# A written issue order for three engines, from the output projection to the FFN's activation sums

## The chip, the core and the metric

The kernel runs on one core of one Trainium2 chip. The core's engines are TensorE (PE: matrix products and transposes into eight PSUM banks of 128 x 512 float32), VectorE (DVE), ScalarE (ACT), GpSimd (POOL), and SyncE (SP), whose queue issues the DMAs. Each engine works through its own list of instructions in order, and semaphores tie the lists together. The metric is the time of one execution on the device in microseconds (us), the median of several runs.

## What is computed

One decoder layer over 1024 tokens of width 1024, in float32. Attention and a gated convolution each give 512 columns; these are normalised, projected, added to x, normalised again and sent through a gated FFN of width 2816. The part around the change:

```python
m = jnp.concatenate([rmsnorm(a, attn_group_norm[i]),
                     rmsnorm(c, conv_group_norm[i])], axis=-1)
x = x + rmsnorm(m @ w_out[i], mix_post_norm[i])
h = rmsnorm(x, ffn_pre_norm[i])
f = (jax.nn.silu(h @ w_gate[i]) * (h @ w_up[i])) @ w_down[i]
x = x + rmsnorm(f, ffn_post_norm[i])
```

with `rmsnorm(x, g) = x * rsqrt(mean(x * x) + 1e-6) * g` over the last axis.

## The kernel before

**Products.** Every float32 matrix is kept as two float32r parts, h (the rounded value, a cast by ScalarE) and l (the rest, a subtraction by VectorE); `split` (L195) makes them. A product is three matmuls per block, h·h, h·l and l·h. So each operand that reaches TensorE costs a ScalarE and a VectorE instruction first. In the FFN, `factor` (L1100) makes the weight's parts for one product and `product` (L1132) is 12 matmuls and the reading of the bank.

**The FFN's seven products.** The FFN's first stage takes the 2x2 blocks of the weights and of the activations and forms seven products in place of eight (Strassen's scheme in Winograd's form). They come in the order p = 1, 2, 6, 5, 7, 3, 4 for each pair fp of weight tiles and for m = 0 (gate) and m = 1 (up). Products 1 and 2 need the activation blocks B11 and B21, which hold the first 512 tokens. Products 3, 5, 6 and 7 need B22 and the sums T1, T2 and T3, which need all tokens; product 4 needs T4. The sums are chained: T3 = B22 - B12, T2 = T3 + B11, T1 = B22 - T2, T4 = B21 - T2. Each is 128 x 2048 and is split when it is done. Products 1 and 2 of fp = 0, 1 and 2 are therefore put ahead of the rest, as work for TensorE while the sums are made.

**The rows before that.** The output projection works on eight tiles t of 128 tokens. For each tile:

- `wo_a` (L1018): 24 matmuls for the attention half (`wo_half`) into two banks; VectorE scales the result and adds the convolution half y, which was written to DRAM earlier (L1021); ScalarE squares the row and sums it (L219, in a helper); the helper `rstd_of` adds epsilon on VectorE (L215) and takes the power -1/2 on GpSimd (L216).
- `wo_x1` (L1025): VectorE normalises (L1027), adds x (L1029); the row is stored to x1_d (L1031); a second square and power for the next norm.
- `wo_n` (L1034): VectorE normalises in place (L1036). As it overwrites the row that is stored to x1_d, it waits until that store has landed.
- `h2_turn` (L1046): TensorE transposes the tile (8 transposes, L1056) into two banks, ScalarE copies them, ScalarE and VectorE split them into B11 and B21 (first four tiles) or B22 (last four). The first four tiles' plain copies go to hr_d in DRAM and are read back later, since T2 and T4 need them; the last four tiles' plain copies stay in `tr`.

The tile loop (L1204) writes these steps staggered: wo_a of tile t, wo_x1 of t - 1, wo_n of t - 2, h2_turn of t - 3.

**Memory.** `mf` is one array of 30 units of 128 x 512 float32. A buffer takes the free units that were freed longest ago; what the last user of the units still does, a new user has to wait for. `raw_load` (L1094) asks for the gate and up weights of one fp and one half. t2, a buffer of its own (four units), holds T2 and then T4, while b12 holds T3.

**What sets the order.** The program is traced into one sequence; the framework's scheduler then gives each engine its list, from a timeline that it reckons itself while compiling, and adds the semaphores. The written sequence is a priority, not an order: an instruction written later may be put ahead on its engine. So it was with the four weight factors that are written at t = 4 (L1237), which were put ahead of the loop.

Of the kernel before, what the change touches and what calls it, by code (L numbers as in the profile page):

```python
# [42 lines left out]
D = 1024  # L43
# [89 lines left out]
def hybrid_layer(ctx: ExitStack, tc: tile.TileContext, x, x_t, p_t, cols_in, positions,  # L133
# [79 lines left out]
    def rstd_of(ss, n=1):  # L213

        dve.tensor_scalar_add(ss, ss, EPS)  # L215
        pool.tensor_tensor(ss, ss, mhalf[:, 0:n], op=ALU.pow)  # L216

    def mean_sq(junk, src, n, ss):
        act.activation(junk, src, AF.Square, scale=float(n) ** -0.5, accum_out=ss)  # L219
# [713 lines left out]
    def wo_half(t, m, k0):  # L933
        ids, b = ps.get(2)
        for n in range(2):
            o = slice(n * U, (n + 1) * U)
            mm3(b[:, o], [(m[j][0].a[:, t * P : (t + 1) * P], m[j][1].a[:, t * P : (t + 1) * P],
                           wo[k0 + j][0].a[:, o], wo[k0 + j][1].a[:, o]) for j in range(4)])
        return ids, b
# [68 lines left out]
        rows_x[t] = mf(2, ML)  # L1008
        sp.dma_start(rows_x[t].a, x[t * P : (t + 1) * P, :])

    def row_norm(t, i):
# [4 lines left out]
        rstd_of(r)

    def wo_a(t):  # L1018
        y = rows_y[t].a
        ids, b = wo_half(t, mTa, 0)  # L1020
        dve.scalar_tensor_tensor(y, b, ss_a[:, t : t + 1], y, op0=ALU.mult, op1=ALU.add)  # L1021
        ps.put(ids)
        row_norm(t, 0)

    def wo_x1(t):  # L1025
        y, xr = rows_y[t].a, rows_x.pop(t)
        dve.scalar_tensor_tensor(y, y, ss_y[:, 2 * t : 2 * t + 1], g_mix.a, op0=ALU.mult,  # L1027
                                 op1=ALU.mult)
        dve.tensor_tensor(y, y, xr.a, op=ALU.add)  # L1029
# [13 lines left out]
    def four(b):  # L1043
        return b.a.rearrange("p (k c) -> p k c", k=4)

    def h2_turn(t):  # L1046
# [5 lines left out]
        for q in range(2):  # L1052
            ids, b = ps.get()
            for j in range(4):
                k = 4 * q + j
                pe.transpose(b[:, j * P : (j + 1) * P], src.a[:, k * P : (k + 1) * P], ident[:])  # L1056
# [4 lines left out]
            if first or q:  # L1061
                h, l = tf["B" + "12"[q] + "12"[not first]]
                split(four(h)[:, :, o], four(l)[:, :, o], bank3(b, 4))
            ps.put(ids)
# [65 lines left out]
    blk, bank = {}, {}  # L1130

    def product(fp, m, p):  # L1132
        key = fp, m, {1: "X", 6: "X", 7: "X", 4: "X", 2: "Z", 5: "Y", 3: "Y"}[p]
# [5 lines left out]
        first, last = p in (1, 2, 5), p in (2, 3, 4)  # L1139
        for k in range(4):  # L1140
            c = slice(k * P, (k + 1) * P)
            pe.matmul(b, wh.a[:, c], th[:, k], start=first and k == 0, stop=False,  # L1142
                      skip_group_check=True)
            pe.matmul(b, wh.a[:, c], tl[:, k], start=False, stop=False, skip_group_check=True)  # L1144
            pe.matmul(b, wl.a[:, c], th[:, k], start=False, stop=k == 3, skip_group_check=True)  # L1145
        free(wh, wl)

        c = {1: "11", 2: "11", 6: "12", 3: "12", 5: "22", 7: "22", 4: "21"}[p]
        if p in (1, 6, 5, 4):
            blk[fp, m, c] = mf(1)  # L1150
        o = blk[fp, m, c].a
        g = blk[fp, 0, c].a
        if p in (1, 6, 5):
            act.copy(o, b)
        elif p == 4 and m == 0:
            act.activation(o, b, AF.Silu)
        elif p == 4:
            dve.tensor_tensor(o, b, g, op=ALU.mult)
        else:
            dve.tensor_tensor(o, b, o, op=ALU.add)  # L1160
            if m == 0:
                act.activation(o, o, AF.Silu)
# [40 lines left out]
    head = [(0, m, p) for p in (1, 2) for m in range(2)]
    for t in range(T + 3):  # L1204
        if t < T:
            wo_a(t)
        elif t == T:
            for d in (mTa, wo):
                for h, l in d.values():
                    free(h, l)  # L1210
            for i in head[:2]:
                product(*i)
        elif t == T + 1:
            for i in head[2:]:
                product(*i)
        if 1 <= t <= T:
            wo_x1(t - 1)
        if t < T:
            load_x(t)
        if 2 <= t <= T + 1:  # L1220
            wo_n(t - 2)
        if t == T + 1:
            free(g_mix, g_ffn)
            t2 = mf(4, MG)
            tf["T1"], tf["T4"] = pair(4, BT), pair(4, BT)
            b11, b21 = tf["T1"][1].a.bitcast(F32), tf["T4"][1].a.bitcast(F32)
            sp.dma_start(b11.rearrange("p (k c) -> p k c", k=4), hr_d[:, 0:4, :])
            sp.dma_start(b21.rearrange("p (k c) -> p k c", k=4), hr_d[:, 4:8, :])
        if t >= 3:
            h2_turn(t - 3)  # L1230
        if t + 2 < T:
            load_y(t + 2)
        if t == T - 1:
            raw_load(0, 1, ML)
        if t == T:
            raw_load(1, 0, ML)
        if t == T // 2:  # L1237
            for i in head:
                factor(*i)
    b12, b22 = tr[0], tr[1]  # L1240
# [14 lines left out]
    t_sum(b12.a, b22.a, b12.a, ALU.subtract)
    both(factor, 1, 1)
    both(product, 1, 1)
    t_sum(t2.a, b12.a, b11, ALU.add)
    t_split("T3", b12.a)
    free(b12)  # L1260
    raw_load(2, 0)
    both(factor, 1, 2)
    both(product, 1, 2)
    t_split("T2", t2.a)
    both(factor, 0, 6)
    t_sum(b22.a, b22.a, t2.a, ALU.subtract)
    both(factor, 2, 1)
    both(product, 2, 1)
    t_split("T1", b22.a)
    free(b22)  # L1270
    both(factor, 2, 2)
    both(product, 2, 2)
# [295 lines left out]
```

## Time and profile before

| | |
|---|---|
| Median of 3 runs | 1228.94 us (1228.4 to 1229.56) |
| The profiled execution: its time, its span from first to last instruction | 1231.37 us, 1229.6 us |
| TensorE busy (matmuls) | 1196.8 us, 97% of the span |
| VectorE busy | 818.5 us, 67% |
| ScalarE busy | 584.8 us, 48% |
| GpSimd busy | 514.6 us, 42% |
| DMA | 215.68 MB, mean 175 GB/s |
| TensorE's granted clock, mean | 0.993 of full speed |

How to read it: the page of a profile lists busy times, the chain of work that ended last and the costliest groups of instructions. The trace behind it can be asked for single stretches of time: a timeline gives start, duration, engine, line of the kernel, what is written and read, and in brackets how long the engine stood idle before and what it waited for. `mem_f` and `mem_r` are the arrays of plain values and of split parts, `banks` is PSUM, `small` holds the row sums. L198 is the cast of `split`, L199 its subtraction, L209 to L211 the projection's matmuls, L1142 to L1145 the FFN's, L1154 to L1164 the reading of the FFN's banks. Matmuls are pipelined, so a matmul that lasts 0.39 us starts 0.23 us after the one before.

The stage of the change lies from about 441 us (the projection's first matmuls) to about 549 us.

### The profile page before, as it was taken

To read this page: it belongs to the slowest core of one execution; us is meant where nothing else is said; L and a number is where in the kernel's file an instruction comes from. 1 tells how busy PE (TensorE), PEld (TensorE's weight loads), DVE (VectorE), ACT (ScalarE), POOL (GpSimd) and SP (SyncE) were. 2 spreads that over 40 slices of the span, in tenths; PEclk is the share of its full clock that TensorE was granted. 3 is DMA by queue.
4 is the path that set the end of the run, shared out by engine and by line. 5 is a ranking of instruction groups with operands and counts; after the bars stand their busy time and mean duration, and the time that the engine had idled before them with its cause. 6 is when DMAs were issued, how large, how long until landed. Compare 5 with 4: busy or idle time off the path is not lost.

```text
span 1229.6 us, 16643 instructions
## 1 busy us (share of the span) xinstructions
PE 1196.8 (97%) x5902; PEld 1009.4 (82%) x5902; DVE 818.5 (67%) x1171; ACT 584.8 (48%) x1071; POOL 514.6 (42%) x391
## 2 busy tenths in 40 slices
PE   7899999999999999889999999999999999999998
PEld 5898888889989887678788888888888888888876
DVE  6954357568866757895757755564657577758675
ACT  6543322357766735643423433333344556545552
POOL 5523545216554312125887745864723012203231
PEclk9999999999999999889999999999999999999999
DMA  6522653894561658624565435534656567654341
GB/s 243 181 70 82 200 205 117 266 380 87 135 164 53 224 195 267 221 103 138 183 226 197 133 133 205 180 126 144 218 189 205 188 216 246 212 189 157 120 141 74
DMA packets 88941, 215.68 MB, mean 175 GB/s; under 512 B 8918, under 2 KB 17402, under 8 KB 87546
## 3 DMA queue, kind: packets, MB, share of 16 engines
q1 hardware_dynamic: 88800, 214.60, 52.5%
q8 instruction: 46, 0.75, 0.3%
q14 instruction: 37, 0.30, 0.1%
q10 hardware_dynamic: 58, 0.02, 0.0%
HBM read 143.28 MB, written 71.04 MB: 174 GB/s over the span
## 4 chain that ended last, share of the span: by engine, by line
PE 78%; DVE 7%; DMA 6%; issue 4%; POOL 2%; ACT 2%; SPq 1%; POOLq 0%; ACTq 0%; DVEq 0%
PE banks L1142 10%; PE banks L1144 10%; PE banks L1145 10%; PE banks L1339 6%; PE banks L1341 6%; PE banks L1340 6%; PE banks L209 5%; PE banks L211 5%; PE banks L210 5%; PE banks L844 2%; DVE mem_r L199 2%; PE banks L815 2%; PE banks L811 1%; PE banks L1451 1%; PE banks L1448 1%
## 5 line engine op out<-in xcount | busy, mean ns | idle before, releaser
L199 DVE TENSOR_TENSOR mem_r<-mem_f,mem_r 128x512 fp32r<-128x512 f32 (+3 forms) x401 | 376.6, 969 | 214.7 <-ACT mem_r L198 201.7
L198 ACT CAST mem_r<-mem_f 128x512 fp32r<-128x512 f32 (+1 forms) x404 | 258.0, 670 | 384.5 <-PE banks L1144 117.9
L1142 PE MATMUL banks<-mem_r 128*128 128x512 f32 x616 | 242.1, 394 | 5.9 <-ACT mem_r L198 5.1
L1144 PE MATMUL banks<-mem_r 128*128 128x512 f32 x616 | 242.2, 393 | 3.0 <-DVE mem_r L199 3.0
L1145 PE MATMUL banks<-mem_r 128*128 128x512 f32 x616 | 241.3, 393 | 0.0
L210 PE MATMUL banks<-mem_r 128*128 128x512 f32 (+2 forms) x536 | 196.6, 368 | 1.4 <-POOL mem_r L199 1.4
L209 PE MATMUL banks<-mem_r 128*128 128x512 f32 (+2 forms) x536 | 195.5, 371 | 1.0 <-DVE small L215 0.4
L211 PE MATMUL banks<-mem_r 128*128 128x512 f32 (+2 forms) x536 | 196.0, 367 | 0.0
L1142 PEld LDWEIGHTS banks<-mem_r 128*128 128x128 f32 x616 | 116.8, 190 | 32.5 <-ACT mem_r L198 6.5
L1144 PEld LDWEIGHTS banks<-mem_r 128*128 128x128 f32 x616 | 117.1, 190 | 27.5 <-DVE mem_r L199 3.5
L1145 PEld LDWEIGHTS banks<-mem_r 128*128 128x128 f32 x616 | 117.0, 190 | 25.1 <-DVE mem_r L199 0.7
L1341 PE MATMUL banks<-mem_r 128*128 128x512 f32 x308 | 119.8, 389 | 0.0
L1339 PE MATMUL banks<-mem_r 128*128 128x512 f32 x308 | 119.8, 390 | 0.0
L1340 PE MATMUL banks<-mem_r 128*128 128x512 f32 x308 | 119.8, 389 | 0.0
L210 PEld LDWEIGHTS banks<-mem_r 128*128 128x128 f32 x536 | 101.2, 189 | 17.9 <-POOL mem_r L199 2.1
L209 PEld LDWEIGHTS banks<-mem_r 128*128 128x128 f32 x536 | 100.7, 189 | 17.7 <-ACT mem_r L198 0.7
L211 PEld LDWEIGHTS banks<-mem_r 128*128 128x128 f32 x536 | 101.0, 189 | 16.1
L829 POOL TENSOR_TENSOR mem_f<-mem_f,stats 128x640 f32<-128x640 f32 (+5 forms) x64 | 72.5, 1146 | 92.2 <-DVE stats L825 45.4
L216 POOL TENSOR_TENSOR small<-small,mhalf 128x1 f32<-128x1 f32 (+2 forms) x42 | 40.8, 972 | 155.3 <-DVE small L215 152.3
L1160 DVE TENSOR_TENSOR mem_f<-banks,mem_f 128x512 f32<-128x512 f32 x66 | 45.2, 686 | 51.5 <-PE banks L1145 51.4
L199 DVE TENSOR_TENSOR mem_r<-banks,mem_r 128x512 fp32r<-128x512 f32 (+3 forms) x118 | 69.2, 612 | 10.9 <-ACT mem_r L198 10.2
L198 ACT CAST mem_r<-banks 128x512 fp32r<-128x512 f32 (+3 forms) x118 | 58.8, 536 | 25.1 <-PE banks L844 13.7
(194 smaller groups left out, 1895.7 us busy)
## 6 DMA issues: line engine op xcount, KB each, us to landing
sc_d<-mem_f SPq DMA_DIRECT2D x77, 256.0 KB, 2.6
mem_f<-sc_d SPq DMA_DIRECT2D x77, 256.0 KB, 3.2
mem_f<-in_w_gate_dram SPq DMA_DIRECT2D x22, 512.0 KB, 5.2
mem_f<-in_w_up_dram SPq DMA_DIRECT2D x22, 512.0 KB, 3.9
mem_f<-in_w_down_dram SPq DMA_DIRECT2D x22, 512.0 KB, 4.2
wc_d<-mem_f SPq DMA_DIRECT2D x22, 512.0 KB, 2.8
mem_f<-wc_d SPq DMA_DIRECT2D x44, 256.0 KB, 3.6
mem_f<-in_w_down_dram SPq DMA_DIRECT2D x33, 256.0 KB, 3.5
```

Source lines behind the costliest of these rows:

```text
L198: act.copy(h, src)
L199: (eng or dve).tensor_tensor(l, src, h.bitcast(F32), op=ALU.subtract)
L209: pe.matmul(o, wh, vh, start=i == 0, stop=False)
L210: pe.matmul(o, wh, vl, start=False, stop=False)
L211: pe.matmul(o, wl, vh, start=False, stop=i == n - 1)
L829: pool.tensor_tensor(pt.a[:, 0:n], pt.a[:, 0:n], sm.to_broadcast([P, n]), op=ALU.mult)
L1142: pe.matmul(b, wh.a[:, c], th[:, k], start=first and k == 0, stop=False, skip_group_check=True)
L1144: pe.matmul(b, wh.a[:, c], tl[:, k], start=False, stop=False, skip_group_check=True)
L1145: pe.matmul(b, wl.a[:, c], th[:, k], start=False, stop=k == 3, skip_group_check=True)
L1339: pe.matmul(b, ah.a[:, c], bh.a, start=first, stop=False, skip_group_check=True)
L1340: pe.matmul(b, ah.a[:, c], bl.a, start=False, stop=False, skip_group_check=True)
L1341: pe.matmul(b, al.a[:, c], bh.a, start=False, stop=last, skip_group_check=True)
```

## The change

From the projection's loop to T4's split, everything stands in one `manual_schedule` region for TensorE, VectorE and ScalarE: their instructions go out in the order in which they are written. GpSimd and SP are scheduled as before. For that the steps are cut into parts that belong to one engine, and written anew as `wo_step`:

```diff
+    def wo_step(t, fill=()):
+        if t < T:
+            wo_mm(t)
+        if t >= 3:
+            turn_act(t - 3)
+        if 1 <= t <= T:
+            wo_a(t - 1)
+        if 2 <= t <= T + 1:
+            row_rstd(t - 2, 1)
+        for i in fill:
+            factor(*i)
+        if t >= 3:
+            turn_dve(t - 3, 0)
+        if 2 <= t <= T + 1:
+            wo_n(t - 2)
+        if 1 <= t <= T:
+            row_rstd(t - 1, 0)
+        if t >= 3:
+            turn_dve(t - 3, 1)
+            turn_put(t - 3)
+        if 2 <= t <= T + 1:
+            turn_pe(t - 2)
+        if 1 <= t <= T:
+            wo_x1(t - 1)
+        if t < T:
+            load_x(t)
+        if t + 2 < T:
+            load_y(t + 2)
```

`wo_mm` is the 24 matmuls; `wo_a` what VectorE does with them and ScalarE's square; `row_rstd` epsilon and power; `turn_pe` the eight transposes; `turn_act` all of ScalarE's copies of a turned tile (for a tile of the first four: two rounded parts, then two plain copies and the store to hr_d; for one of the last four: one rounded part and two plain copies); `turn_dve` the subtraction of one of its two banks; `wo_x1` ends with ScalarE's second square. The four factors of fp = 0, p = 1 and 2, are the `fill` of steps 4 to 7, one each. `product` is cut into its matmuls (`product_mm`) and the reading of the bank (`product_end`). What follows the loop is written out:

```diff
+        for t in range(T):
+            wo_step(t, {4: ((0, 0, 1),), 5: ((0, 1, 1),), 6: ((0, 0, 2),), 7: ((0, 1, 2),)}
+                    .get(t, ()))
...
+        raw_load(0, 1, ML)
+        both(product_mm, 0, 1)
+        wo_step(T)
+        raw_load(1, 0, ML)
+        both(product_end, 0, 1)
...
+        both(product_mm, 0, 2)
+        wo_step(T + 1)
+        free(g_mix, g_ffn)
+        raw_load(2, 0, ((0, 22),))
+        product_end(0, 0, 2)
+        factor(1, 0, 1)
+        product_mm(1, 0, 1)
+        factor(1, 1, 1)
+        product_end(0, 1, 2)
+        product_mm(1, 1, 1)
+        factor(0, 0, 6)
+        turn_act(T - 1)
+        turn_dve(T - 1, 1)
+        turn_put(T - 1)
+        both(product_end, 1, 1)
+        b12, b22 = tr[0], tr[1]
+        t_sum(b12.a, b22.a, b12.a, ALU.subtract)
+        factor(1, 0, 2)
+        product_mm(1, 0, 2)
+        factor(1, 1, 2)
+        product_mm(1, 1, 2)
+        t_split("T3", b12.a)
+        factor(2, 0, 1)
+        product_end(1, 0, 2)
+        product_mm(2, 0, 1)
+        t_sum(b12.a, b12.a, b11, ALU.add)
+        factor(2, 1, 1)
+        product_mm(2, 1, 1)
+        product_end(1, 1, 2)
+        t_split("T2", b12.a)
+        both(product_end, 2, 1)
+        factor(2, 0, 2)
+        product_mm(2, 0, 2)
+        factor(2, 1, 2)
+        product_mm(2, 1, 2)
+        factor(0, 1, 6)
+        t_sum(b22.a, b22.a, b12.a, ALU.subtract)
+        product_end(2, 0, 2)
+        t_split("T1", b22.a)
+        product_end(2, 1, 2)
+        free(b22)
+        both(factor, 0, 5)
+        t_sum(b12.a, b21, b12.a, ALU.subtract)
+        factor(0, 0, 7)
+        t_split("T4", b12.a)
```

The sums: t2 is gone; b12 holds T3, then T2, then T4, each written over the one before. The four units that t2 had are free, and raw_load(2, 0) stands ahead of the sums, where before it stood behind T3's split. raw_load(0, 1) moves from tile T - 1 to behind the loop, raw_load(1, 0) from tile T to behind step T.

More of the change, by code (lines that the diff above doesn't have):

```diff
@@ L1044, in four, with turn_pe, turn_places, turn_act @@
         return b.a.rearrange("p (k c) -> p k c", k=4)
-    def h2_turn(t):
+    turned = {}
+    def turn_pe(t):
         src = rows_y.pop(t)
-        o = slice(t % 4 * P, (t % 4 + 1) * P)
+        turned[t] = [ps.get(), ps.get()]
+        for q, (ids, b) in enumerate(turned[t]):
+            for j in range(4):
+                k = 4 * q + j
+                pe.transpose(b[:, j * P : (j + 1) * P], src.a[:, k * P : (k + 1) * P], ident[:])
+        free(src)
+    def turn_places(t):
+        o = slice(t % 4 * P, (t % 4 + 1) * P)
+        for q, (ids, b) in enumerate(turned[t]):
+            if t < T // 2 or q:
+                h, l = tf["B" + "12"[q] + "12"[t >= T // 2]]
+                yield q, b, four(h)[:, :, o], four(l)[:, :, o]
+    def turn_act(t):
+        o = slice(t % 4 * P, (t % 4 + 1) * P)
+        for q, b, h, l in turn_places(t):
+            act.copy(h, bank3(b, 4))
         first = t < T // 2
@@ L1051, in h2_turn @@
             raw = mf(2, ML)
[L1052 to L1056, printed above, removed]
+        for q, (ids, b) in enumerate(turned[t]):
             if first:
@@ L1060, in h2_turn @@
                 act.copy(four(tr[q])[:, :, o], bank3(b, 4))
[L1061 to L1064, printed above, removed]
         if first:
@@ L1067, in h2_turn, with turn_dve, turn_put @@
             free(raw)
-        free(src)
+    def turn_dve(t, only):
+        for q, b, h, l in turn_places(t):
+            if q == only:
+                dve.tensor_tensor(l, bank3(b, 4), h.bitcast(F32), op=ALU.subtract)
+    def turn_put(t):
+        for ids, b in turned.pop(t):
+            ps.put(ids)
     for t in range(NW, T):
@@ L1138, in product @@
         th, tl = (four(v) for v in tf[RIGHT[p]])
-        first, last = p in (1, 2, 5), p in (2, 3, 4)
+        first = p in (1, 2, 5)
         for k in range(4):
@@ L1146, in product, with product_end @@
         free(wh, wl)
+    def product_end(fp, m, p):
+        key = (fp, m, {1: "X", 6: "X", 7: "X", 4: "X", 2: "Z", 5: "Y", 3: "Y"}[p])
+        ids, b = bank[key]
         c = {1: "11", 2: "11", 6: "12", 3: "12", 5: "22", 7: "22", 4: "21"}[p]
@@ L1164, in product @@
                 dve.tensor_tensor(o, o, g, op=ALU.mult)
-        if last:
+        if p in (2, 3, 4):
             ps.put(ids)
@@ L1202, in hybrid_layer @@
     tr[0], tr[1] = mf(4, ((22, 26),)), mf(4, ((26, 30),))
[L1203 to L1240, printed above, removed]
     def both(f, fp, p):
@@ L1253, in t_sum @@
         dve.tensor_tensor(o, x, y, op=op)
[L1255 to L1272, printed above, removed]
@@ new lines, in hybrid_layer @@
+    EN = mybir.EngineType
+    with tc.manual_schedule(engines={EN.PE, EN.DVE, EN.Activation}):
+        for t in range(T):
+            wo_step(t, {4: ((0, 0, 1),), 5: ((0, 1, 1),), 6: ((0, 0, 2),), 7: ((0, 1, 2),)}
+                    .get(t, ()))
+        for d in (mTa, wo):
+            for h, l in d.values():
+                free(h, l)
+        raw_load(0, 1, ML)
[3 more added lines that the diff above has]
+        both(product_end, 0, 1)
+        tf["T1"], tf["T4"] = pair(4, BT), pair(4, BT)
+        b11, b21 = tf["T1"][1].a.bitcast(F32), tf["T4"][1].a.bitcast(F32)
+        sp.dma_start(b11.rearrange("p (k c) -> p k c", k=4), hr_d[:, 0:4, :])
+        sp.dma_start(b21.rearrange("p (k c) -> p k c", k=4), hr_d[:, 4:8, :])
+        both(product_mm, 0, 2)
[43 more added lines that the diff above has]
+        t_split("T4", b12.a)
+        free(b12)
```

25 lines of the change are left out of this document (13 added, 12 removed).

## The prediction

> **What bounds the kernel now.** First the window view over the stages that the change touches: stretch, us, each engine's busy time (TensorE, its weight loads, VectorE, ScalarE, GpSimd), TensorE's granted clock, DMA share and GB/s.
>
> ```profile
> 441.00:488.00 47.00, 47.00 (x228) 39.29 (x227) 36.16 (x47) 19.44 (x37) 10.49 (x12) 1.00 0.65 209
> 488.00:535.00 47.00, 36.66 (x147) 28.57 (x146) 40.40 (x47) 28.62 (x46) 5.03 (x5) 0.85 0.50 180
> 535.00:549.00 14.00, 14.00 (x63) 11.56 (x62) 11.31 (x12) 7.53 (x11) 3.42 (x3) 1.00 0.30 106
> ```
>
> TensorE never stops during the output projection (441 to 488) nor from 535 on. Between, it is busy 36.66 of 47 us at a clock of 0.85. What ended the stops is in TensorE's timeline and the view of waits (total, times, longest); how it ran after them, in the window view again:
>
> ```profile
> 485.66 0.39 PE L209 MATMUL banks<-mem_r 128*128 128x512 f32 x1
> ...
> 487.48 0.39 PE L211 MATMUL banks<-mem_r 128*128 128x512 f32 x1
> 489.51 0.73 PE L1142 MATMUL banks<-mem_r 128*128 128x512 f32 x2 [0.76 <-ACT mem_r L198]
> ...
> 528.70 0.79 PE L1142 MATMUL banks<-mem_r 128*128 128x512 f32 x1 [3.08 <-ACT mem_r L198]
> ```
> ```profile
> PE banks L1144 <- DVE mem_r L199: 3.0, 1, 3.0
> PE banks L1056 <- DVE mem_f L1036: 2.2, 1, 2.2
> ```
> ```profile
> 493.30:496.50 3.20, 3.20 (x8) 2.52 (x9) 3.20 (x4) 1.15 (x2) 0.00 (x0) 0.50 0.38 108
> 510.90:513.80 2.90, 2.90 (x7) 2.22 (x8) 2.90 (x5) 2.52 (x5) 0.00 (x0) 0.51 0.46 184
> 528.70:534.20 5.50, 5.50 (x13) 4.33 (x14) 5.50 (x5) 2.68 (x3) 0.00 (x0) 0.50 0.00 0
> ```
>
> Eight matmul starts from 485.66 to 487.48 make 0.228 us each. After each stop of 2 to 3 us the clock stood at half: 28 matmuls in 11.6 us, 6.4 at full clock. After the stop of 0.76 us it did not (two in 0.73). Idle 10.3, half-clock stretches 5.2 and ragged restarts (an estimate of 1.5) make **17 us lost**. That is all the change can win: 1229 - 17 = 1212.
>
> VectorE's timeline shows the kind of fault:
>
> ```profile
> 491.93 0.69 DVE L1112 TENSOR_TENSOR mem_f<-mem_f 128x512 f32<-128x512 f32 x1 [3.00 <-DMA mem_f<-in_w_gate_dram]
> 492.54 0.68 DVE L199 TENSOR_TENSOR mem_r<-banks,mem_r 128x512 fp32r<-128x512 f32 x1
> ```
>
> The subtraction at 492.54, for which TensorE stood 3.0 us, sat behind a factor's sum that waited for a weight. An engine does nothing past its next instruction. The new order is just as fixed, so I read it for the same fault.
>
> **The change part by part.** The instructions are the same, the four sums too; order and places change. I walk the three written lists with durations from these rows: timelines of VectorE, ScalarE and GpSimd, groups with their mean ns, the DMA view and x1_d's landings, TensorE's chain.
>
> ```profile
> 439.98 2.50 DVE L199 TENSOR_TENSOR mem_r<-mem_f,mem_r 128x512 fp32r<-128x512 f32 x4 [5.09 <-ACT mem_r L198]
> ...
> 446.31 1.28 DVE L1021 SCALAR_TENSOR_TENSOR mem_f<-banks,small,mem_f 128x1024 f32<-128x1024 f32 x1 [2.43 <-PE banks L211]
> 448.81 0.16 DVE L215 TENSOR_SCALAR small<-small 128x1 f32<-128x1 f32 x1 [1.22 <-ACT mem_r L219]
> 449.63 1.28 DVE L1027 SCALAR_TENSOR_TENSOR mem_f<-mem_f,small 128x1024 f32<-128x1024 f32 x1 [0.66 <-DMA y_d<-mem_f]
> 450.95 1.23 DVE L1029 TENSOR_TENSOR mem_f<-mem_f 128x1024 f32<-128x1024 f32 x1
> ...
> 455.92 1.28 DVE L1036 SCALAR_TENSOR_TENSOR mem_f<-mem_f,small 128x1024 f32<-128x1024 f32 x1 [1.18 <-DMA x_d<-mem_f]
> ...
> 481.51 1.28 DVE L199 TENSOR_TENSOR mem_r<-banks,mem_r 128x512 fp32r<-128x512 f32 x2
> ```
> ```profile
> 464.26 1.06 ACT L219 ACTIVATE mem_r<-mem_f 128x1024 fp32r<-128x1024 f32 x1 [2.29 <-DVE mem_f L1029]
> ...
> 468.17 0.22 ACT L219 ACTIVATION_READ_ACCUMULATOR mem_r<-mem_f 128x1 f32 x1
> ```
> ```profile
> 481.68 0.54 POOL L216 TENSOR_TENSOR small<-small,mhalf 128x1 f32<-128x1 f32 x1 [3.33 <-DVE small L215]
> ```
> ```profile
> L199 DVE TENSOR_TENSOR mem_r<-mem_f,mem_r 128x512 fp32r<-128x512 f32 x17 | 11.6, 704 | 0.1
> L198 ACT CAST mem_r<-mem_f 128x512 fp32r<-128x512 f32 x15 | 9.0, 620 | 13.6 <-PE banks L1144 8.1 <-DMA mem_f<-in_w_up_dram 3.5 <-DVE mem_f L1118 1.7
> L1154 ACT COPY mem_f<-banks 128x512 f32<-128x512 f32 x8 | 4.6, 581 | 4.0 <-PE banks L1145 4.0
> L1160 DVE TENSOR_TENSOR mem_f<-banks,mem_f 128x512 f32<-128x512 f32 x6 | 4.1, 685 | 1.9 <-PE banks L1145 1.9
> L1162 ACT ACTIVATE mem_f<-mem_f 128x512 f32<-128x512 f32 x3 | 1.9, 629 | 0.3 <-DVE mem_f L1160 0.3
> L1162 ACT ACT_TABLE_LOAD x1 | 1.3, 1283 | 0.0
> ```
> ```profile
> x_d<-mem_f SPq DMA_DIRECT2D x8, 512.0 KB, 4.6
> ```
> ```profile
> DMA to landing us min/median/max: 2.6/4.1/6.8
> ```
> ```profile
> 515.68 0.87 PE banks L1056 x8
> ```
>
> *A plain step of the loop.* Zero is the end of wo_x1's addition (L1029; 452.18 for row tile 0). Its store to x1_d must land before wo_n overwrites the row: wo_n began at 455.92, 3.74 later. In the new order only wo_a, an epsilon addition and at most one subtraction stand between on VectorE, so the wait is not filled. Then wo_n 1.28; the epsilon addition, GpSimd's power and the start of wo_x1 0.82 (448.81 to 449.63), begun 0.08 before wo_n's end, as VectorE's neighbours overlap; wo_x1's two instructions 2.55 (449.63 to 452.18). 3.74 + 1.28 - 0.08 + 0.82 + 2.55 = **8.3 us**. The power keeps its 0.54 beside a subtraction that reads a bank (481.51 and 481.68 ran together), which is what stands there.
>
> *A step that also makes a factor* (t = 4 to 7). ScalarE has in this order: the square of the x1 row, four copies of the turned tile, the square of wo_a's row, the factor's cast. The same six took 464.26 to 468.39, 4.13. Begun 0.03 after zero, less 0.10 of overlap, the cast runs 4.06 to 4.68. The factor's subtraction is next on VectorE after the epsilon addition, so VectorE idles from 1.4 to 4.7, and turn_dve (long ready) and wo_n queue behind: 4.71 + 0.60 + 0.60 + 1.28 = 7.19; then - 0.08 + 0.82 + 2.55: **10.5 us**. At t = 7 one copy and one subtraction fewer: **9.4**. Before, these four subtractions lay at 439.98, ahead of the projection, where they cost nothing.
>
> TensorE needs 24 x 0.228 + 0.87 = 6.3 us a step, and turn_pe stands after wo_mm and waits for wo_n: VectorE's list sets the pace. Step 1 is as before and ends at 452.18. Steps 2, 3 and 8 at 8.3, 4 to 6 at 10.5, 7 at 9.4 lead to 517.9; the last wo_n ends 3.74 + 1.28 later, 523.0. This has the 3.6 us landing of the first store throughout. The median here is 4.6, which I take in steps 3, 8 and 9 (beside the last two run weight loads and the reads of hr_d): + 3. So the last transposes end at 526.9; before, at 516.6. From 446.1, when wo_mm(0) is through, TensorE's work until then is 168 projection matmuls and 48 products at 0.228 and 64 transposes (7.0): 56.2 of 80.8 us. **Lost: 24.6.**
>
> *After the loop* 96 products of p = 1 and 2 remain, with no transposes between, and three hand-offs stop TensorE. (a) The cast of factor (1,0,1) stands on ScalarE behind the SiLU of (0,0,2), whose addition stands behind the last wo_n and a subtraction: 0.6 + 0.6 + 0.63 + 0.5 against 0.9 of transposes: 1.5; 2.8 if the table load isn't done while ScalarE idles before it (I take it done: there are over 2 us). (b), (c) The casts of (1,0,2) and of (2,0,2) stand behind the copies of both products before them: 0.2 + 0.58 + 0.62 = 1.4 each. A stretch at half clock after (a), which follows another stop and transposes, as the one at 510.90 did: 1.5. None after (b) and (c), whose 1.4 I put nearer to the 0.76 that stayed fast than to 2 to 3; else + 3.
>
> [...]
>
> Losses: 24.6 + 1.5 + 1.5 + 2.8 = 30.4, less 17: **+13 us**. It is made against the profiled span (1229.6; that execution took 1231.4 in all), 0.1% from the median, so I put it on the median: 1228.94 + 13 = **1242**.
>
> *At no cost.* The shared place: the next sum now waits until T3 is split, but stands behind that on VectorE anyway. The room lets raw_load(2,0) go ahead of T3's split, which removes the 3.08 us stop at 528.70; its second transfer waits for the last transposes and lands about 4 us later, some 8 us before its factor; without that cover the 3 us are back. raw_load(0,1) and (1,0) move behind the loop on SP's queue; their places are free by about 510 and they are read after 528. x and y rows are asked for a step or more ahead.
>
> **The rivals.** *Faster.* VectorE's own work in a factor step is 1.20 + 0.07 + 0.60 + 0.60 + 1.20 + 0.07 + 0.60 + 1.20 + 1.14 = 6.7 us, near TensorE's 6.3. Were its waits covered by steps that run into each other, TensorE would lose only the hand-offs, 5.8 of the 17: 1229 - 11 = 1218. For it: before, the same work kept TensorE going without a stop to 488. Against: that order mixed three tiles, while this one has the store's landing inside every turn. It decides at a step under 6.3.
> *No change.* The order isn't binding, or the stops it removes pay for those it makes: 1229, at steps of about 7.
> *Much slower.* A store waits on SP behind a row load that itself waits for hr_d:
>
> ```profile
> SPq L1005 <- DMA hr_d<-mem_f: 8.4, 3, 3.8
> ```
>
> Up to 3.8 us in two or three plain steps, or three landings at 6.8: 7 to 12 more, 1249 to 1254.
>
> **How the numbers follow.** Forecast 0.66, much slower 0.14, faster 0.12, no change 0.08. Landings of 2.6 for 4.6 take 6 from the sum; the table load, two more such stretches and landings 1 us later add 7: 1236 to 1249 for the forecast itself. The range adds the slower rival, and goes down to 1231 since the walk may price some waits twice: 1231 to 1254, which leaves out the faster case and part of no change. About 0.2%, 2.5 us, can be told from nothing: faster 0.13, same 0.08, slower 0.79.
>
> **What would show it.** Right: VectorE idle some 3 us before L199 (from mem_f) in four steps, and before wo_n on x_d in the others; wo_a 8 to 10 us apart; TensorE stopped 2 to 4 us before the transposes from 465 on and 1.4 us before two products; the last transposes near 527; no stop on in_w_up. Wrong: TensorE without a stop to 500, or wo_a 6 to 7 us apart.

## The result, and the profile after

The changed kernel takes 1251.64 us (median of four runs, 1248.13 to 1252.42) beside 1229.2 us (1228.4 to 1229.56) for the kernel before. The ratio is 1.0169, 95% interval 1.0151 to 1.0187: slower by 22 us, where 13 were forecast. The time lies in the range, near its upper end. The profiled execution after took 1252.35 us with a span of 1250.0, so the two spans differ by 20.4 us.

The window view of the kernel after, for the stretches shown of before and one more (columns as there):

```profile
441.00:488.00 47.00, 40.59 (x188) 33.26 (x187) 29.38 (x38) 17.56 (x33) 6.55 (x10) 0.93 0.60 196
488.00:535.00 47.00, 35.91 (x152) 28.33 (x151) 30.52 (x40) 22.86 (x43) 3.79 (x7) 0.89 0.61 202
535.00:549.00 14.00, 12.70 (x44) 9.85 (x44) 12.31 (x11) 6.26 (x7) 0.00 (x0) 0.76 0.05 19
549.00:575.00 26.00, 22.72 (x90) 17.46 (x89) 19.78 (x21) 12.79 (x19) 1.99 (x1) 0.93 0.09 31
```

Before, TensorE ran without a stop to 488 and again from 535. Now it stops in the first stretch (188 matmul starts for 228) and is not through with its stops at 575. What it waited for from 441 to 660, in the view of waits (total, times, longest), and after that the same view for VectorE from 441 to 535:

```profile
PE banks L1060 <- DVE small L215: 15.7, 6, 4.0
PE banks L1172 <- ACT mem_r L198: 2.8, 3, 1.6
PE banks L1175 <- DVE mem_r L199: 2.7, 3, 1.3
PE banks L1172 <- DVE mem_f L1194: 1.4, 1, 1.4
PE banks L1174 <- DVE mem_r L199: 1.1, 1, 1.1
```
```profile
DVE mem_r L199 <- ACT mem_r L198: 14.1, 5, 3.3
DVE mem_f L1042 <- DMA x_d<-mem_f: 8.0, 3, 4.6
```

L1060 is the transposes, L215 an epsilon addition of VectorE that stands just behind wo_n (L1042) in its list: six stops ahead of the transposes, 15.7 us. The stop of 3.08 us for a weight of raw_load(2,0) is gone. VectorE stands 14.1 us for casts and 8.0 us for the store of the x1 row. Its timeline shows where:

```profile
467.44 1.23 DVE L1035 TENSOR_TENSOR mem_f<-mem_f 128x1024 f32<-128x1024 f32 x1
468.58 1.28 DVE L1027 SCALAR_TENSOR_TENSOR mem_f<-banks,small,mem_f 128x1024 f32<-128x1024 f32 x1
469.94 0.15 DVE L215 TENSOR_SCALAR small<-small 128x1 f32<-128x1 f32 x1
473.43 0.69 DVE L199 TENSOR_TENSOR mem_r<-mem_f,mem_r 128x512 fp32r<-128x512 f32 x1 [3.33 <-ACT mem_r L198]
...
477.95 1.22 DVE L1035 TENSOR_TENSOR mem_f<-mem_f 128x1024 f32<-128x1024 f32 x1
...
515.62 1.28 DVE L1042 SCALAR_TENSOR_TENSOR mem_f<-mem_f,small 128x1024 f32<-128x1024 f32 x1 [4.56 <-DMA x_d<-mem_f]
```

From one end of wo_x1 (L1035) to the next, 468.67 to 479.17, are 10.5 us. In them VectorE, with its subtraction of the factor next in its list, waits 3.33 us for the cast, and wo_n, turn_dve and wo_x1 wait behind it. At 515.62 wo_n waits 4.56 us for the landing of the store.

Below, "lost" is the time of TensorE between one matmul's start and the next beyond 0.228 us (0.112 for a transpose), summed over a stretch; stops and half-clock stretches both fall into it. "To the transposes" is from 441 us to the end of the last transposes of the output projection (516.6 us before, 526.9 after, each kernel's own end in its row). The kernels e1 to e15 are those of the experiments, told below.

| kernel | median us | lost to the transposes | from there to 575 | 575 to 660 | sum |
|---|---|---|---|---|---|
| before | 1229 to 1231 | 11.5 | 6.7 | 1.3 | 19.6 |
| after | 1251.64 | 23.8 | 12.9 | 2.4 | 39.0 |
| e1_factors_first | 1246.29 | 17.2 | 12.3 | 2.9 | 32.4 |
| e2_own_row | 1245.14 | 17.8 | 9.5 | 6.0 | 33.4 |
| e3_handoffs | 1251.51 | 23.6 | 8.6 | 7.2 | 39.4 |
| e4_room_only | 1229.25 | 14.2 | 3.6 | 3.9 | 21.7 |
| e5_no_region | 1227.15 | 7.1 | 8.2 | 0.0 | 15.3 |
| e6_loop | 1235.12 | 7.6 | 13.1 | 3.2 | 23.9 |
| e8_both | 1237.89 | 8.0 | 11.2 | 5.4 | 24.6 |
| e9_handoffs_gp | 1246.27 | 24.4 | 7.7 | 3.7 | 35.8 |
| e10_all | 1229.19 | 6.4 | 10.9 | 0.1 | 17.3 |
| e12_free_pool | 1235.75 | 7.4 | 14.9 | 2.2 | 24.4 |
| e13_dve_free | 1244.18 | 23.3 | 6.4 | 1.3 | 30.9 |
| e15_act_free | 1252.77 | 24.6 | 7.8 | 8.5 | 40.9 |

After minus before, 39.0 - 19.6 = 19.4 us, are nearly the whole 20.4; 1.2 us of the rest had come by 427 us, before anything that was changed.

### The profile page after: what moved, and what is told of

Same layout as the page of the kernel before. It is cut to its first block, busy times and chain, and to the rows that moved or that the text cites. A ratio compares the mean times of both kernels' runs of the same rounds, so it can differ in the third digit from the quotient of the medians.

```text
span 1250.0 us, 16611 instructions
## 1 busy us (share of the span) xinstructions
PE 1205.9 (96%) x5902; PEld 1014.9 (81%) x5902; DVE 821.7 (66%) x1171; ACT 583.8 (47%) x1071; POOL 511.2 (41%) x391
## 4 chain that ended last, share of the span: by engine, by line
PE 71%; DVE 10%; DMA 7%; POOL 5%; ACT 3%; issue 3%; SPq 0%; POOLq 0%; DVEq 0%; ACTq 0%
PE banks L1172 8%; PE banks L1175 8%; PE banks L1174 8%; PE banks L1407 6%; PE banks L1405 6%; PE banks L1406 6%; PE banks L209 5%; PE banks L211 5%; PE banks L210 5%; PE banks L844 2%; DVE mem_r L199 2%; PE banks L815 1%; PE banks L811 1%; PE banks L1517 1%; PE banks L1516 1%
## 5 line engine op out<-in xcount | busy, mean ns | idle before, releaser
L199 DVE TENSOR_TENSOR mem_r<-mem_f,mem_r 128x512 fp32r<-128x512 f32 (+3 forms) x401 | 383.0, 985 | 219.5 <-ACT mem_r L198 209.7
L210 PE MATMUL banks<-mem_r 128*128 128x512 f32 (+2 forms) x536 | 198.6, 371 | 0.8 <-DVE mem_r L202 0.7
L209 PE MATMUL banks<-mem_r 128*128 128x512 f32 (+2 forms) x536 | 197.9, 376 | 1.3 <-DVE small L215 0.4
L211 PE MATMUL banks<-mem_r 128*128 128x512 f32 (+2 forms) x536 | 198.0, 371 | 0.0
L1172 PEld LDWEIGHTS banks<-mem_r 128*128 128x128 f32 x616 | 117.0, 190 | 31.2 <-ACT mem_r L198 4.1
L1175 PEld LDWEIGHTS banks<-mem_r 128*128 128x128 f32 x616 | 117.2, 190 | 29.2 <-DVE mem_r L199 4.5
L1174 PEld LDWEIGHTS banks<-mem_r 128*128 128x128 f32 x616 | 117.1, 190 | 25.7 <-DVE mem_r L199 1.5
L209 PEld LDWEIGHTS banks<-mem_r 128*128 128x128 f32 x536 | 102.1, 192 | 18.2 <-ACT mem_r L198 1.0
L210 PEld LDWEIGHTS banks<-mem_r 128*128 128x128 f32 x536 | 102.8, 192 | 17.4 <-DVE mem_r L202 1.0
L211 PEld LDWEIGHTS banks<-mem_r 128*128 128x128 f32 x536 | 102.7, 192 | 16.6
L216 POOL TENSOR_TENSOR small<-small,mhalf 128x1 f32<-128x1 f32 (+2 forms) x42 | 36.6, 871 | 172.0 <-DVE small L215 169.4
L1406 PEld LDWEIGHTS banks<-mem_r 128*128 128x128 f32 x308 | 57.8, 188 | 12.0
L1407 PEld LDWEIGHTS banks<-mem_r 128*128 128x128 f32 x308 | 57.8, 188 | 12.0
```

The lines of the kernel that those rows point to most:

```text
L199: (eng or dve).tensor_tensor(l, src, h.bitcast(F32), op=ALU.subtract)
L209: pe.matmul(o, wh, vh, start=i == 0, stop=False)
L210: pe.matmul(o, wh, vl, start=False, stop=False)
L211: pe.matmul(o, wl, vh, start=False, stop=i == n - 1)
L1406: pe.matmul(b, ah.a[:, c], bl.a, start=False, stop=False, skip_group_check=True)
L1407: pe.matmul(b, al.a[:, c], bh.a, start=False, stop=last, skip_group_check=True)
```

## The experiments

The ratios are to the kernel before on the same chip (medians 1230.66, 1230.58 and 1229.91 us in the three lots). Each edit is to the kernel after, unless it says otherwise.

**The factors ahead of the loop.** The four `fill` factors go ahead of the loop, inside the region.

```diff
+        for p in (1, 2):
+            both(factor, 0, p)
         for t in range(T):
-            wo_step(t, {4: ((0, 0, 1),), 5: ((0, 1, 1),), 6: ((0, 0, 2),), 7: ((0, 1, 2),)}
-                    .get(t, ()))
+            wo_step(t)
```

> The changed kernel with the four weight factors of fp = 0 written ahead of the loop and no longer in steps 4 to 7; nothing else differs. Theory (the factor's cast stands on ScalarE behind two squares and four copies, and VectorE's list behind its subtraction): steps 4 to 6 fall from 10.5 us to the plain step's 8 or so and step 7 from 9.4, in all some 8 us; TensorE waits on that pace, so 1244 us against 1251.6. The subtractions from mem_f leave the loop, and what VectorE then waits for before wo_n is x1_d's store. Rival 1 (the store's landing sets the pace of these steps too, and the factor hides in it): within 3 us, 1249 to 1252. Rival 2 (VectorE is short of time in the loop, not waiting): only the four subtractions' 2.4 us, 1249.

Measured: 1246.29 us, ratio 1.0132 (1.0115 to 1.0149). The steps from one end of wo_x1 to the next were 7.5, 7.8, 8.7, 8.6, 8.8, 10.6 and 9.1 us, where after has 7.5, 7.8, 10.5, 10.5, 10.5, 9.4 and 10.5. So the time lies between the theory's 1244 and the rivals' 1249: the first three steps that had held a factor became 1.7 to 1.9 us shorter, for the 2.5 expected, and the fourth grew from 9.4 to 10.6. VectorE's largest wait in the loop, of this kernel:

```profile
DVE mem_f L1042 <- DMA x_d<-mem_f: 13.4, 7, 4.6
```

The casts' wait is gone (14.1 to 1.2), but the store's has grown from 8.0 to 13.4: in a factor step the store landed while VectorE stood for the cast.

**The normalized row in its own place.** wo_n writes to a new buffer, so nothing waits for the store of x1.

```diff
-        y = rows_y[t].a
-        dve.scalar_tensor_tensor(y, y, ss_y[:, 2 * t + 1 : 2 * t + 2], g_ffn.a, op0=ALU.mult,
+        y, n = rows_y[t], mf(2, ML)
+        dve.scalar_tensor_tensor(n.a, y.a, ss_y[:, 2 * t + 1 : 2 * t + 2], g_ffn.a, op0=ALU.mult,
                                  op1=ALU.mult)
+        free(y)
+        rows_y[t] = n
```

> The changed kernel with wo_n writing into a buffer of its own, so that it no longer waits for the landing of x1_d's store; the factors stay in steps 4 to 7. Theory (in those steps ScalarE's list is the longer wait): only the plain steps gain: steps 2 and 3 about 0.5 us each, step 8 (10.5 us, a late landing) some 3, the last wo_n some 1.5; steps 4 to 7 keep 10.5 and 9.4. In all 5 us: 1246 to 1247. Rival (the store's landing inside each turn sets the pace of the whole loop): seven steps fall to some 7.5, 17 us less, 1235.

Measured: 1245.14 us, ratio 1.0122 (1.0105 to 1.0140). The steps were 6.6, 7.8, 10.5, 10.5, 10.5, 9.4 and 7.1: only the first and the last, two of the three without a factor, got shorter. The time is near the theory's 1246, far from the rival's 1235. The store's wait is gone, the casts' stays to a tenth, VectorE's waits again:

```profile
DVE mem_r L199 <- ACT mem_r L198: 14.1, 5, 3.3
```

**Casts and subtractions ahead of the bank copies.** After the loop the factors (1,m,2), (2,m,2) and (0,m,5) go ahead of product_end and of the sums of that stage, T1's sum and split forward too.

```diff
         product_mm(1, 1, 1)
+        both(factor, 1, 2)
         factor(0, 0, 6)
...
-        factor(1, 0, 2)
         product_mm(1, 0, 2)
-        factor(1, 1, 2)
...
+        both(factor, 2, 2)
         t_split("T2", b12.a)
         both(product_end, 2, 1)
-        factor(2, 0, 2)
         product_mm(2, 0, 2)
-        factor(2, 1, 2)
         product_mm(2, 1, 2)
-        factor(0, 1, 6)
         t_sum(b22.a, b22.a, b12.a, ALU.subtract)
-        product_end(2, 0, 2)
+        factor(0, 1, 6)
         t_split("T1", b22.a)
+        both(factor, 0, 5)
+        product_end(2, 0, 2)
         product_end(2, 1, 2)
         free(b22)
-        both(factor, 0, 5)
```

> The changed kernel with the order after the loop rewritten: the casts and subtractions of factors (1,m,2), (2,m,2) and (0,m,5) stand ahead of the bank copies and sums, and the sum for T1 and its split ahead of the reading of the last products. The loop is as it was. Theory (the stops after the last transposes come from factors that queue behind bank copies and 2.3 us sums): of the 11.8 us that TensorE loses between 526.6 and 575 some 8 go: 1243 to 1244. Rival (VectorE has no room there, so that moving instructions only moves the stops): within 2 us of 1251.6.

Measured: 1251.51 us, ratio 1.0174 (1.0154 to 1.0194). The rival held, my theory did not: nothing gained. The table shows how: 4.5 us less lost up to 575, 4.8 more after it. The stop that took them, in TensorE's waits from 575 to 660, and GpSimd's timeline just ahead of it, both of this kernel:

```profile
PE banks L1172 <- ACT mem_r L198: 3.9, 1, 3.9
```
```profile
570.90 1.30 POOL L1138 TENSOR_TENSOR mem_f<-mem_f 128x512 f32<-128x512 f32 x1 [48.57 <-ACT mem_r L198]
...
604.57 1.29 POOL L1138 TENSOR_TENSOR mem_f<-mem_f 128x512 f32<-128x512 f32 x1 [4.12 <-DMA mem_f<-in_w_gate_dram]
```

GpSimd, which makes the weight sums of the FFN's pairs from fp = 1 on, has nothing to do for 48.57 us, begins pair 1 at 570.9 and, after a load, the next pair at 604.57; TensorE then waits, from 613.8, for factors made of those sums. In after GpSimd begins at 573.0 and 604.15. From this came a new theory: TensorE can't be sooner there than GpSimd, so what is saved after the loop is only waited for later.

**The same with less for GpSimd to do.** The weight sums of the down projection for fp = 0, 1 and 2 (four sums each on GpSimd) are put three pairs later; the edit before this one is kept.

```diff
-        if p == 5 and m == 1:
+        if p == 5 and m == 1 and fp > 2:
             w_factors(fp)
+        if p == 7 and m == 1 and 3 <= fp < 6:
+            w_factors(fp - 3)
```

> The kernel with its casts and subtractions ahead of the bank copies after the loop, which gained nothing, and besides it the down projection's weight sums of the first three FFN pairs (GpSimd, four sums of 1.7 us a pair) done some pairs later, where GpSimd has room. New theory for why the hand-offs gained nothing: GpSimd is without work from 523 to 571, then sums without a pause to 600 and after a load from 604.6 on, and TensorE at 613.8 to 618.7 waits for factors made from those sums; so TensorE sooner through the hand-offs only waits longer there. By it the stops of 4.05 and 0.76 us at 613 to 619 go and the time is 1244 to 1247 us. Rival (that stop comes from VectorE's or the loads' side): the stop stays and the time is 1250 to 1253 us.

Measured: 1246.27 us, ratio 1.0125 (1.0106 to 1.0143), 5 us less than without it. GpSimd's timeline, where the next pair now begins 7.3 us sooner:

```profile
597.25 1.28 POOL L1138 TENSOR_TENSOR mem_f<-mem_f 128x512 f32<-128x512 f32 x1 [0.60 <-DMA mem_f<-in_w_up_dram]
```

The new theory held. The stop at 613.8 is gone; one of 2.0 us at 590 is there. So the stops after the loop do cost time, but only together with GpSimd's late start does taking them out show. The later weight sums by themselves were not run; all that after loses beyond 575 is 2.4 us.

**Shared place and early load alone.** The kernel before, scheduled as before, with t2 gone and raw_load(2,0) ahead of the sums.

```diff
-            t2 = mf(4, MG)
+            raw_load(2, 0, ML)
...
-    t_sum(t2.a, b12.a, b11, ALU.add)
     t_split("T3", b12.a)
-    free(b12)
-    raw_load(2, 0)
+    t_sum(b12.a, b12.a, b11, ALU.add)
```

(and b12 for t2 in the lines that follow)

> The kernel before, scheduled as before, with only the second part of the change: T3, T2 and T4 share one place, t2 is gone, and raw_load(2,0) stands ahead of the sums. Theory (the 3.08 us stop at 528.7 and the half-clock stretch after it come from the late load): 5 to 6 us less, 1224. Rival (the scheduler's order puts another wait there): within 2 us of 1229.

Measured: 1229.25 us, ratio 0.9992 (0.9981 to 1.0004). The stop of 3.08 us at 528.7 is gone, but the time isn't better: the rival held. TensorE's waits of this kernel:

```profile
PE banks L1056 <- DVE mem_f L1036: 4.5, 1, 4.5
PE banks L1144 <- DVE mem_r L199: 3.1, 1, 3.1
PE banks L1142 <- DVE mem_f L1160: 2.0, 1, 2.0
```

Before, the first of these was 2.2 us and the third 0.5: the scheduler made another order around the new place, and the stops in it are as long as the one that went. The shared place costs nothing, as forecast; that it saves the 3 us was wrong.

**The text without the order.** The region is taken out; the new text is only the scheduler's priority.

```diff
-    with tc.manual_schedule(engines={EN.PE, EN.DVE, EN.Activation}):
+    if True:
```

> The same text as after, but the three engines' order isn't fixed: the text is only the priority by which the scheduler of before orders them. My theory (a fixed order puts a waiting instruction ahead of ready ones on VectorE, and the waits add up): the scheduler moves ready work ahead, the 3.3 us that VectorE sits before the factors' subtractions goes or moves off the row tiles' path, and the time falls to between 1227 and 1238 us. Rival (it is the new text, what each step holds and which products come when, that costs, whether the order is fixed or not): 1245 us or more, steps of 9 to 10.5 us in the middle of the loop as in after.

Measured: 1227.15 us, ratio 0.9974 (0.9964 to 0.9983). My theory held. The text, the steps and the places are the same, and the time is 24 us shorter: all of the slowdown comes from the order being fixed. The window view:

```profile
441.00:488.00 47.00, 47.00 (x225) 39.28 (x224) 35.84 (x47) 22.11 (x40) 9.49 (x12) 1.00 0.65 218
488.00:535.00 47.00, 40.54 (x190) 32.88 (x188) 39.06 (x51) 29.46 (x48) 4.98 (x5) 0.96 0.52 189
```

TensorE doesn't stop until 491 and is busy 40.54 us of the next 47, beside 36.66 before and 35.91 after. This kernel beats both, though the one before by 0.26% only.

**VectorE alone freed, ScalarE alone freed.** Which engine's written list is it?

```diff
-    with tc.manual_schedule(engines={EN.PE, EN.DVE, EN.Activation}):
+    with tc.manual_schedule(engines={EN.PE, EN.Activation}):
```
```diff
-    with tc.manual_schedule(engines={EN.PE, EN.DVE, EN.Activation}):
+    with tc.manual_schedule(engines={EN.PE, EN.DVE}):
```

> After with only TensorE and ScalarE in the written order; VectorE is left to the scheduler. With all three left to it the time was 1227. Theory (VectorE's written list sets the loop's pace, since it holds both waits: the factors' subtractions for ScalarE's cast, and the normalization for the store's landing): VectorE goes on with another tile in both waits, steps near 7.8, the length of ScalarE's written list; 1232 to 1240 us. Rival (what costs is ScalarE's order, which puts the factor's cast behind four copies and a square): 1244 to 1252 us.

> The counterpart: after with TensorE and VectorE in the written order, ScalarE left to the scheduler. Theory: ScalarE casts the factors as soon as their weights are there, so the 3.3 us before VectorE's four subtractions go, but the wait for the store's landing stays in VectorE's list: steps of 8 to 9 us as with the factors ahead of the loop, 1241 to 1247 us, slower than the run with VectorE free. Rival (ScalarE's order alone is the cause): below 1238 us and faster than with VectorE free.

Measured: 1244.18 us, ratio 1.0119 (1.0101 to 1.0138), with VectorE free; 1252.77, ratio 1.0187 (1.0167 to 1.0206), with ScalarE free. Both theories and the second rival missed; the first rival's time came (1244), but not for its reason, since freeing ScalarE gave nothing. In the loop neither run won anything to speak of: 23.3 and 24.6 us lost to the transposes, for 23.8. With VectorE free, ScalarE's waits from 462 to 527 are

```profile
ACT mem_r L219 <- DVE mem_f L1035: 34.0, 6, 9.2
```

(33.5 in after). ScalarE's list has the square of the x1 row (L219) first and the tile's copies, the other square and the cast behind it, so all of them still wait for wo_x1, and the next wo_x1 needs the other square, which ends 4.2 us after the wo_x1 before it (470.75 to 474.97). In the list that the scheduler then made for VectorE, wo_n, which still waits for the store (6.1 us in five waits), and the tile's subtractions often stand ahead of the epsilon addition as well. The steps are 9 to 10 us, one 13, and TensorE still stops ahead of the transposes:

```profile
PE banks L1060 <- DVE mem_f L1042: 17.1, 7, 3.7
```

With ScalarE free, VectorE's waits:

```profile
DVE mem_f L1042 <- DMA x_d<-mem_f: 23.3, 8, 6.0
```

The casts come early, and the store's wait goes from 8.0 to 23.3: steps of 9.2 to 9.7, the last 12.0. What the run with VectorE free did win, 7.5 us, came after the loop (6.4 us lost to 575 for 12.9, and 1.3 after that for 2.4). So the loop's loss is not in one list: the lists of VectorE and ScalarE hold each other, and freeing one leaves the other's wait. Two things stay open: TensorE's list was fixed in both runs and not tried by itself, and another order for the freed engine than the scheduler's might have won more.

**Both waits out.** The edits of e1_factors_first and e2_own_row together.

> After with the first two of these four changes alone: four factors ahead of the loop, and the normalized row in its own place. Done singly they gave 5 and 6.5 us. Theory: each step had two waits in a row and either alone leaves the other, so together they give more than their sum: the step is ScalarE's square, four copies and square with VectorE's work behind them, 7.8 us as in the one step without factor and store that was seen; last transposes near 509, time 1234 us. Rivals: they add, 1240 us; or a pin after the loop, above 1240 us.

Measured: 1237.89 us, ratio 1.0059 (1.0039 to 1.0078), between theory and first rival. The loop did what the theory said: steps 6.6, 7.8, 7.9, 7.9, 7.9, 8.0, 7.1, the last transposes end at 509.5, and 15.8 us less are lost up to there than in after (by the two singly 6.6 and 6.0, together 12.6). 3 us of it were lost again after 575, most of them at 595, where GpSimd is late as in e3_handoffs: the cast that TensorE's stop goes back to waited for one of its sums.

```profile
595.75 0.62 ACT L198 CAST mem_r<-mem_f 128x512 fp32r<-128x512 f32 x1 [2.86 <-POOL mem_f L1140]
```

**The loop with ScalarE's list turned round.** Besides these two, the square of wo_a's row ahead of the tile's copies, and turn_dve a step later (turn_pe takes its two banks as a pair for that).

```diff
-        if t >= 3:
-            turn_act(t - 3)
         if 1 <= t <= T:
             wo_a(t - 1)
+        if t >= 3:
+            turn_act(t - 3)
...
-        if t >= 3:
-            turn_dve(t - 3, 0)
+        if t >= 4:
+            turn_dve(t - 4, 0)
```

> After with the four factors ahead of the loop, the normalized row in a place of its own (no store to wait for), the square of wo_a's row ahead of the turned tile's copies on ScalarE, and the turned tile's subtractions one step later on VectorE. Theory (the loop's step is VectorE's list, waits included): what is left is VectorE's own work, near 6.5 us a step beside TensorE's 6.3, so TensorE hardly stops until the last transposes, which end at 503 to 506 instead of 526.9; the time is 1251.5 - 22 = 1229 us, if what is lost after the loop stays. Rival (something after the loop pins the time, so that a loop sooner through only waits longer there): the loop is as short, but the time stays above 1236 us, with more stops after 530.

Measured: 1235.12 us, ratio 1.0035 (1.0018 to 1.0053), between the two. Steps: 6.6, 6.6, 7.2, 9.1, 8.0, 8.2, 6.6. The three steps of 6.6 are VectorE's own work as expected; in the others there is a wait that no kernel had before. VectorE's waits, and SP's queue from 455 to 505:

```profile
DVE mem_f L1035 <- DMA mem_f<-in_x_dram: 6.2, 4, 2.5
```
```profile
SPq L1009 <- DMA hr_d<-mem_f: 9.3, 4, 4.0
```

The loads of the x rows stand on SP until the tile copy that had their place is stored to hr_d, and now the row is wanted sooner. The last transposes ended at 511.1 instead of 503 to 506.

**All of it, in written order.** The edits of e6_loop, e3_handoffs and e9_handoffs_gp.

> All three engines in written order, with every wait that was found taken out: factors ahead of the loop, the normalized row in its own place, the square ahead of the copies, the tile's subtractions a step later (together 1235.1), the casts and subtractions ahead of the bank copies after the loop, and GpSimd's weight sums later (these two together took 5.3 off after). Theory: the terms add, 1230 us, about as before. Rivals: the later part has no work left to hide in once the loop is shorter, 1233 to 1236; or what the loop lost to late rows of x (6 us, since the new place takes theirs) is hidden too, 1225.

Measured: 1229.19 us, ratio 0.9994 (0.9984 to 1.0004). The terms add, as expected. A written order with every wait found taken out is as good as the scheduler's before, and not better.

**The sums on GpSimd.** To e5_no_region:

```diff
     def t_sum(o, x, y, op):
-        dve.tensor_tensor(o, x, y, op=op)
+        pool.tensor_tensor(o, x, y, op=op)
```

> No engine's order fixed (the kernel that took 1227.2), and besides it the four sums of the activation blocks (128x2048, 2.3 us each on VectorE) go to GpSimd, which has nothing to do from 501 to 550. In that kernel VectorE works without a pause from 521 to 540 and TensorE stops there for 5.2 us in two stops. Theory: VectorE's load is what stops TensorE there; with 9 us of it gone the stops go, 1220 to 1224 us. Rival: a sum of this size on GpSimd is slow (three to four times a 512 sum of 1.3 us) and the two engines slow each other (VectorE's 512 subtraction took 0.68 us with GpSimd idle and 1.2 to 1.8 beside GpSimd's sums), so the chain of sums ends later and T2 is late: 1227 us or more.

Measured: 1235.75 us, ratio 1.0051 (1.0034 to 1.0068). The rival held, for more than its reason. The timelines of VectorE and GpSimd, and TensorE's longest wait from 500 to 560:

```profile
520.09 3.60 DVE L199 TENSOR_TENSOR mem_r<-mem_f,mem_r 128x512 fp32r<-128x512 f32 x1
...
528.22 9.60 DVE L199 TENSOR_TENSOR mem_r<-mem_f,mem_r 128x512 fp32r<-128x512 f32 x2
```
```profile
518.52 4.62 POOL L1248 TENSOR_TENSOR mem_f<-mem_f 128x2048 f32<-128x2048 f32 x1 [12.00 <-ACT mem_f L1082]
527.78 4.60 POOL L1248 TENSOR_TENSOR mem_f<-mem_f,mem_r 128x2048 f32<-128x2048 f32 x1 [4.63 <-DVE mem_r L199]
532.45 4.82 POOL L1248 TENSOR_TENSOR mem_f<-mem_f 128x2048 f32<-128x2048 f32 x1
```
```profile
PE banks L1172 <- ACT mem_r L198: 9.6, 1, 9.6
```

A sum takes GpSimd 4.6 us for VectorE's 2.28, and meanwhile VectorE's subtractions, 0.68 us each, don't end: the one begun at 520.09 ends at 523.69, 0.55 after GpSimd's sum; the two from 528.22 take 9.60, the length of two sums. The work meant to leave VectorE held it instead.

## Why the prediction was right, and where not

**What bounds it: right.** The 17 us lost before are 19.6 when small gaps are counted too and the count goes on to 660 us.

**The loop's steps: right.** A factor step was put at 10.5 us and took 10.5 three times; the step at t = 7 was put at 9.4 and took 9.4. Its cause is as argued, in ScalarE's timeline after:

```profile
468.76 1.06 ACT L219 ACTIVATE mem_r<-mem_f 128x1024 fp32r<-128x1024 f32 x1 [3.74 <-DVE mem_f L1035]
...
472.77 0.63 ACT L198 CAST mem_r<-mem_f 128x512 fp32r<-128x512 f32 x1
```

The plain steps, put at 8.3, took 7.5 and 7.8 where the store landed in 2.8 us, and 10.5 in the last (with a landing of 5.9); the two errors are 1.3 too much and 2.2 too little, beside the 3 us put on for landings. The last transposes end at 526.93 (forecast 526.9), and 23.8 us are lost by then (24.6). That the end is met to the tenth is luck: the kernel was 1.2 us late before the loop began, which was not in the forecast, and the loop itself was as much shorter than forecast. That it is the fixed order, and not the new text, is shown by e5_no_region.

**VectorE's list sets the pace: half wrong.** The walk followed both lists and came out right, but the words named one engine. Freed alone, neither VectorE nor ScalarE cut the loop's loss by more than 0.5 us (e13_dve_free, e15_act_free). The two waits lie beside each other in time, as e1, e2 and e8 show.

**After the loop: the step that was mis-sized.** Forecast were three hand-offs, 1.5, 1.4 and 1.4 us, and 1.5 of half clock: 5.8. Measured are 12.9 us to 575 and 2.4 after, 15.3. (a) cost 0.4 and no half clock (granted 1.00 from 527 to 534): the table load (1.28 us at 523.84, the SiLU at 525.95) was done beforehand, as I took it, and the cast came sooner. At (b) the cast came after 1.8 us, about as forecast, but TensorE stopped again for 1.5, for a subtraction. VectorE's timeline there:

```profile
533.82 2.28 DVE L1248 TENSOR_TENSOR mem_f<-mem_f 128x2048 f32<-128x2048 f32 x1
536.02 1.29 DVE L199 TENSOR_TENSOR mem_r<-mem_f,mem_r 128x512 fp32r<-128x512 f32 x2
```

The factor's subtraction stands behind the activation sum. The walk asked only for the cast. Then the clock stood at half, where the forecast had put "none after (b) and (c)" (its "else + 3" would have met this one). (c) cost 1.1. The two stops at 562 and 565, 1.3 and 1.2 us, were not seen at all: T1's low part, and a factor's subtraction behind it on VectorE. After them too the clock stood at half. Both stretches in the window view:

```profile
537.00:542.50 5.50, 5.50 (x14) 4.24 (x15) 4.27 (x5) 1.96 (x3) 0.00 (x0) 0.50 0.00 0
566.90:569.90 3.00, 3.00 (x9) 2.32 (x8) 3.00 (x3) 0.37 (x1) 0.00 (x0) 0.50 0.05 17
```

Of the 12.9 us the six stops are 7.2, these two stretches about 2.8 and 1.4, and ragged restarts the rest. The 1.6 us at 613.8 are GpSimd's late start.

**The sum.** Forecast 24.6 + 5.8 - 17 = 13.4. Measured 23.8 + 15.3 - 19.6 = 19.4 (before rounding), with 1.2 from the late start 20.6, for a difference of spans of 20.4. The sign came from the first term. The second was 9.5 us short; the larger loss before (2.6) and the loop's (0.8) took some of that back, the late start added its 1.2, and 7 us were missing.

**At no cost: right in size.** No stop on a weight of raw_load(2,0), and nothing for the place (e4_room_only); but there the stop removed did not pay, as others came.

**The rivals.** The faster one needed steps under 6.3. With all its waits covered the written loop came to 6.6 in three steps (e6_loop). The slower one's time was met, 1249 to 1254, but not its mechanism: the x1 stores went out as wo_x1 ended, and one landing, not three, was late (5.9 us). The forecast itself was put at 1236 to 1249; the measured 1251.64 lies in the stated range only by the part that was added for this rival, and that is luck.

## What to carry to other kernels

In an engine's written list, ask of each instruction what it waits for and what that has queued ahead of it, for each engine that feeds it: the casts were walked here and the subtractions were not, and three stops for subtractions (1.5, 1.3 and 1.2 us) with the two half-clock stretches behind them were missed. A wait that is taken out shows its worth only if nothing else ends at the same time: waits that lie beside each other have to be taken out together, and the next engine to be late (here GpSimd) has to be looked up beforehand. A fixed order over several engines should be tried against the same text as a mere priority; that one line was worth 24 us.

## What the runs showed of the hardware

**Stops of one length, with and without half clock.** TensorE's timeline at the same place in e8_both and then in e2_own_row, after a stop of 2.71 us each:

```profile
598.15 0.50 PE L1174 MATMUL banks<-mem_r 128*128 128x512 f32 x1 [2.71 <-DVE mem_f L1196]
598.49 0.39 PE L1176 MATMUL banks<-mem_r 128*128 128x512 f32 x1
```
```profile
607.77 0.80 PE L1174 MATMUL banks<-mem_r 128*128 128x512 f32 x1 [2.71 <-DVE mem_f L1196]
608.36 0.63 PE L1176 MATMUL banks<-mem_r 128*128 128x512 f32 x1
...
610.91 0.40 PE L1176 MATMUL banks<-mem_r 128*128 128x512 f32 x1
```

The one goes on at full clock (granted 1.00 from 598.2 to 602), the other at half for 3 us (from 608.36 to 610.49 a start every 0.43 us and 0.63 us a matmul, for 0.23 and 0.39 in the one; granted 0.70 from 607.8 to 613). A pair of stops does the same: 1.27 and 1.17 us at 562 and 565 in after were followed by half clock (0.50 from 566.9 to 569.9), 1.27 and 1.18 us ahead of the same products in e8_both (544 and 546) were not (1.00 from 527 to 551). So the length of a stop alone doesn't decide it, and the price of one of 2 to 3 us can only be given as a range: from the stop's end on, seven matmul starts took 1.73 us in e8_both and 3.14 in e2_own_row, 0.1 and 1.5 more than at 0.228. What does decide it, no run here shows.

**VectorE beside GpSimd's sums.** In e12_free_pool the three VectorE subtractions of 128x512 with operands in `mem_f` and `mem_r` that began during GpSimd's first three sums ended 0.55 us after them (3.60, 4.70 and 4.98 us, for 0.68 at 538.95 with GpSimd idle), while an addition that reads a bank took 0.69 us beside such a sum (at 519.48). In after, beside GpSimd's sums of 1.7 us, the two kinds stand next to each other on VectorE:

```profile
580.98 0.68 DVE L1194 TENSOR_TENSOR mem_f<-banks,mem_f 128x512 f32<-128x512 f32 x1
581.59 1.18 DVE L199 TENSOR_TENSOR mem_r<-mem_f,mem_r 128x512 fp32r<-128x512 f32 x1
```

The subtraction ends at 582.77, 0.55 us after GpSimd's sum of 1.63 us that began at 580.59. I had it in the expectation as mutual slowing, not as a hold.
